# Diagonal blocks of a chunked RWKV-7 scan: one strided transfer instead of sixteen, and the triangular steps on GpSimd instead of VectorE

## The chip, the cores and the metric

The kernel runs on one core of one Trainium2 chip, as a single program. The metric is the device time of one execution in microseconds (us). A core has five engines with queues of their own: TensorE (PE in the profile, its weight loads PEld), VectorE (DVE), ScalarE (ACT), GpSimd (POOL) and SyncE (SP, which here only issues transfers). Each engine takes its instructions strictly in the order in which they stand in its queue; an instruction that has to wait for a semaphore holds everything behind it on that engine. Transfers are issued by SP, ACT or POOL and moved by 16 DMA engines.

## The reference

A decoder trunk of two layers on 512 tokens and 16 learned meta tokens, width 1024. Each layer is: half-step SwiGLU block, a mixer (a 31-tap convolution branch beside an RWKV-7 branch, both gated), a second half-step SwiGLU block, each followed by a LayerNorm. What the change touches is the RWKV-7 scan in the mixer, 16 heads of size 64:

```python
def step(S, inp):
    r_t, w_t, k_t, v_t, kk_t, a_t = inp
    sa = jnp.einsum("bhvk,bhk->bhv", S, -kk_t)
    S = (S * w_t[:, :, None, :]
         + sa[..., None] * (kk_t * a_t)[:, :, None, :]
         + v_t[..., None] * k_t[:, :, None, :])
    y = jnp.einsum("bhvk,bhk->bhv", S, r_t)
    return S, y
...
_, ys = lax.scan(step, S0, xs)
```

The state S of a head is 64x64; every token applies a rank-one correction to it and adds a rank-one term. All numbers are float32.

## The kernel before

The scan is computed in chunks of 64 tokens (`C`, eight of them, `NCH`) and a first chunk of the 16 meta tokens (`NM`). Inside a chunk the corrections of the tokens depend on each other through a 64x64 triangular matrix with ones on its diagonal, one for each head and chunk, and its inverse is needed before the chunk can be scanned.

The 16 heads go in four quarters (`q`) of four heads, and a quarter's 32 matrices in two halves (`g`) of four chunks, 16 matrices each. For a quarter the work is:

- `prep` projects and prepares the operands of two pairs of heads.
- `scores` makes, chunk by chunk on PE (L1345, L1354), the matrices. ACT copies the triangular part to the tile `ut` (L1359), and SP writes it to a scratch tensor `mscr` in DRAM (L1366).
- `substitution(q, g)` inverts the 16x16 diagonal blocks of a half: four per matrix, 64 in all (68 in the first half, with the meta chunk's), one on each partition. SP fetches them from `mscr` to the tile `im` (L1380), DVE does 15 columns with one multiplication (L1389, into `is`) and one addition (L1392, on `ix`) each, 30 dependent instructions. ACT copies the transposed result to `it` (L1396). SP writes both to `xdscr` in DRAM (L1398) and fetches them back into the block diagonals of `dd` (L1403), 16 transfers of 8 KB: two forms, four blocks, two groups of partitions. What lies beside the blocks in `dd` was set to zero once per layer (L1143).
- `inverse(q, g)` puts the 64x64 inverses together on PE from `ut` and `dd` (16 products at L1428, then three rounds of 16 at L1435, with DVE between), and ACT copies them to `G` (L1442).
- `scan(q)` goes through the eight chunks (L1510 to L1545). While it runs, the scores of the next quarter are made, and with them the first half's `substitution` of that quarter. That quarter's first `inverse` comes after the scan, its second one at the start of its own scan.

So each layer has eight substitutions and eight inverses. The four first halves of a layer are called the "first-half places" below, eight in the kernel. They have the short way from scores to inverse; the second halves are needed only when the next scan begins.

PE is kept busy between these steps by other products of the mixer, projections of 264 columns each (`mm` at L250, 48 of them to a projection); the text calls them fill. DVE has the convolution's taps (`cacc`, L1183) and the splitting of weights (`w_lo`, L164) as its own filling work. POOL sets tiles and issues the accumulating transfers of part of the weight splits (L158 in the mixer).

The order of the instructions on each engine is made when the program is built, by a scheduler that takes them by priority and by the times it expects of them. The priorities of taps and scores are shifted by `high_priority`; otherwise nothing in the code fixes where on PE an inverse stands. `nosync` adds an order without a wait; `self.hold` is the instruction that the next tap has to come after in that order.

Of the kernel before, what the change touches and what calls it, by code (L numbers as in the profile page):

```python
# [11 lines left out]
ALU = mybir.AluOpType  # L12
# [4 lines left out]
P = 128  # L17
# [3 lines left out]
NM = 16  # L21
# [8 lines left out]
HS = 64  # L30
C = 64
NCH = SEQ // C
LN_EPS = 1e-5
GN_EPS = 64e-5
ALPHA = (2 * DEPTH) ** 0.25
# [72 lines left out]
class Trunk:  # L108
# [686 lines left out]
    def mixer(self, l, last, pre, more):  # L795
        nc, tc = self.nc, self.tc
        self.l, self.last = l, last
        self.t0, self.n = (NM, SEQ // 2) if last else (0, T // 2)
        dram = lambda name, shape: self.dp.tile(shape, F32, name=f"{name}{l}")
# [3 lines left out]
        self.gs = dram("gscr", [2 * D, T])  # L803
        self.us = dram("uscr", [D, T])
        self.ds, self.as_, self.ggs = dram("dscr", [D, T]), dram("ascr", [D, T]), dram("ggscr", [D, T])
        self.ms = dram("mscr", [4, NCH * 4, C, C])
        self.ms0 = dram("mscr0", [4, 4, NM, NM])
        self.xs0 = dram("xscr0", [4, 4, NM, NM])
        self.xd = dram("xdscr", [4, 2, 2, P // 2, NM, NM])
        ppool, self.pp = self.enter(f"mix_ps{l}", space=PSUM)  # L810
        pms = [self.mm() for _ in range(2)]
        self.glu0 = self.sc()
# [55 lines left out]
        N = prep(1)  # L868
        post = iter(())
        self.cuts = CUTS  # L870
        for q in range(4):
# [42 lines left out]
            Q, N = N, prep(q + 2) if q < 2 else None  # L914
# [147 lines left out]
    def mixer_begin(self, zs, filler):  # L1062

        nc, mp, d = self.nc, self.mp, self.d
        z = self.tmp()
        self.token_mix(zs[0], 24, z)
        nc.scalar.activation(z[0:64, :], z[0:64, :], AF.Tanh)
        x = self.tmp("kp", 1, F32R), self.tmp("k2", 1, F32R)  # L1070
        self.split(z, *x)
        z = self.tmp()
        self.token_mix(zs[1], 25, z)
        nc.scalar.activation(z, z, AF.Tanh, scale=0.5)
        xg = self.tmp("a", 1, F32R), self.tmp("pinv", 1, F32R)
        nc.scalar.activation(xg[0], z, AF.Copy, bias=1.0)
        nc.vector.scalar_tensor_tensor(xg[1], z, 1.0, xg[0].bitcast(F32), op0=ALU.add,
                                       op1=ALU.subtract)
        filler(START[0])
        acts = (lambda o: (AF.Sigmoid, self.v1("w0", o), 1.0),  # L1080
                lambda o: (AF.Tanh, self.half[:, 0, o:o + 1], 0.5))
        up = [(d["w_up"], slice(0, 64)), (d["a_up"], slice(64, P))]

        room = mp.tile([P, 4, KT, P], F32R, name="sb", bufs=1)
        w = self.wunit(*((r, u[self.l].rearrange("r (o c) -> r o c", c=P)) for u, r in up),
                       dst=[room[:, 0], room[:, 1]])

        self.bi = 0
        stage = {}

        def lowrank(w, x, o, r, dst, act=None):
            if act is None:
                t = self.tmp("v", 4) if o % 2 else mp.tile([P, NCH * 4, 32], F32, name="b4",
                                                           bufs=B4)
                t = t if o % 2 else t.rearrange("p a b -> p (a b)")[:, 0:T]
            else:
                if o == 0:
                    stage[r.start] = self.rows().rearrange("p q e f t -> p (q e f) t")
                t = stage[r.start][:, o]
            both = self.sc() if self.bi % 2 == 0 else None  # L1100
            self.bi += 1
            for h in range(2):
                s = slice(h * (T // 2), (h + 1) * (T // 2))
                pm = (self.sm(("tr", "ch")[h]) if both is None else both[:, h])[:, :T // 2]
                for j, (a, b) in enumerate(((0, 0), (0, 1), (1, 0))):
                    nc.tensor.matmul(pm, w[a][r, o, :], x[b][r, s], start=j == 0, stop=j == 2)
                to = t[:, s]
                if both is not None:
                    if h == 0:
                        continue  # L1110
                    pm, to = self.pv(both), self.tv(t)
                if act is None:
                    nc.vector.tensor_scalar_mul(to, pm, 0.5)
                else:
                    f, b, scale = act(o)
                    nc.scalar.activation(to, pm, f, bias=b, scale=scale)
            nc.sync.dma_start(out=dst[o * P:(o + 1) * P, :], in_=t)

        wg = self.wunit(d["g_up"][self.l].rearrange("r (o c) -> r o c", c=P),
                        dst=[room[:, 2], room[:, 3]])  # L1120
        todo = [[lambda o=o, r=r, act=act, dst=dst: lowrank(w, x, o, r, dst, act)
                 for o in range(KT)]
                for (_, r), act, dst in zip(up, acts, (self.ds, self.as_))]
        todo.append([lambda o=o: lowrank(wg, xg, o, slice(0, P), self.ggs) for o in range(KT)])
        for i, (j, o) in enumerate(LOW):
            todo[j][o]()
            if i % LOWSTEP == LOWSTEP - 1:
                filler(1)
            self.taps(TAP0[0])
        filler(START[1])  # L1130
        self.sb = mp.tile([P, NCH, 4, 2 * C], F32, name="sb", bufs=1)

        self.ut = mp.tile([P, NCH * 2, C], F32, name="ut")

        small = mp.tile([P, 2048], F32, name="small")
        nc.gpsimd.memset(small, 0.0)
        self.small, o = {}, 0
        for name, n in (("kb", 512), ("s", 256), ("v", 256), ("u", 256), ("y0", 256), ("y1", 256), ("y2", 256)):
            self.small[name] = small[:, o:o + n]
            o += n  # L1140

        self.dd = mp.tile([P, NCH * 2, 2, C], F32, name="dd")
        nc.gpsimd.memset(self.dd, 0.0)  # L1143


    def glu_b(self, ct):
# [162 lines left out]
    def scores(self, q, Q):  # L1309


        nc, mp = self.nc, self.mp
# [13 lines left out]
        for e in range(2):  # L1326
            p0 = ps[e][0:NM, 0:4 * 2 * NM].rearrange("a (p f x) -> a p f x", p=2, f=2)
            r = slice(HS * e, HS * e + HS)
            for p in range(2):
                for f in range(2):  # L1330
# [7 lines left out]
                              in_=s0[0:NM, e, :, 1, 0, :])  # L1338
        yield
        for c in range(NCH):  # L1340
# [8 lines left out]
            U = self.ut[C * (c % 2):C * (c % 2) + C, 4 * (c // 2):4 * (c // 2) + 4, :]  # L1349
            pairs = []  # L1350
            for p in range(2):
                for e in range(2):
                    r = slice(HS * e, HS * e + HS)
# [9 lines left out]
            nc.vector.tensor_tensor(G[0:C, :, :, 0, cs].rearrange("a p e t -> a e p t"),  # L1363
                                    pv[0:C, :, :, 0, :], mask[0:C, 0], op=ALU.mult)
            to = 4 * (4 * (c // 4) + 2 * (c % 2) + c % 4 // 2)
            nc.sync.dma_start(out=self.ms[q, to:to + 4].rearrange("h j t -> j h t"), in_=U)  # L1366
            yield

    def substitution(self, q, g, Q):


        nc, mp, dd = self.nc, self.mp, self.dd
        N = NCH * 2
        blocks = [slice(NM * b, NM * b + NM) for b in range(4)]
        np_ = 4 * N + (4 if g == 0 else 0)
        M, X, XT = (mp.tile([P, NM, NM], F32, name=x, bufs=2)[0:np_] for x in ("im", "ix", "it"))
        nc.gpsimd.memset(X, 0.0)
        nc.gpsimd.memset(X.rearrange("s t i -> s (t i)")[:, 0::NM + 1], 1.0)
        for b, r in enumerate(blocks):
            nc.sync.dma_start(out=M[b * N:(b + 1) * N], in_=self.ms[q, g * N:(g + 1) * N, r, r])  # L1380
        if g == 0:
            nc.sync.dma_start(out=M[4 * N:], in_=self.ms0[q])
        steps = []
        for j in range(NM - 1):
            w, k = NM - 1 - j, j + 1
            y = mp.tile([P, 64], F32, name="is", bufs=2)[0:np_, 0:w * k]
            y = y.rearrange("s (t i) -> s t i", t=w)
            x = X[:, j + 1:, 0:k]
            steps.append(nc.vector.tensor_tensor(  # L1389
                y, M[:, j, j + 1:, None].to_broadcast([np_, w, k]),  # L1390
                X[:, j, None, 0:k].to_broadcast([np_, w, k]), op=ALU.mult))
            steps.append(nc.vector.tensor_tensor(x, x, y, op=ALU.add))  # L1392
        for later, earlier in zip(steps[1:], steps):
            self.nosync(later, earlier)
        self.hold = steps[-1]
        nc.scalar.copy(XT, X.rearrange("s t i -> s i t"))  # L1396
        for f, x in enumerate((X, XT)):
            nc.sync.dma_start(out=self.xd[q, g, f], in_=x[0:4 * N])  # L1398
            for b, r in enumerate(blocks):
                for e in range(2):  # L1400
                    o = C * e + NM * b
                    k = b * N + e * N // 2
                    nc.sync.dma_start(out=dd[o:o + NM, g * N // 2:(g + 1) * N // 2, f, r],  # L1403
                                      in_=self.xd[q, g, f, k:k + N // 2]
                                      .rearrange("s t i -> t s i"))
        if g == 0:
            nc.sync.dma_start(out=self.xs0[q], in_=XT[4 * N:])
            xt0 = mp.tile([P, 64], F32, name="xt", bufs=1)[0:NM].rearrange("a (s t) -> a s t", s=4)
            nc.sync.dma_start(out=xt0, in_=self.xs0[q].rearrange("s i t -> i s t"))
            Q["xt0"] = xt0  # L1410
# [401 lines left out]
```

## Time and profile before

| | |
|---|---|
| median of 3 runs | 3013.95 us (3011.65 to 3015.38) |
| the profiled execution | 3008.79 us, its span 3007.1 us |
| mean granted PE clock in it | 0.994 |
| PE busy | 2936.7 us, 98% of the span |
| DVE busy | 2272.8 us, 76% |
| ACT busy | 1417.0 us, 47% |
| POOL busy | 181.4 us, 6% |
| the two mixers | about 400 to 960 us and 1910 to 2490 us |

A view of groups gives busy time, mean duration and what ended the idle time ahead of the group. A timeline row has start and duration in us, engine, line, operation, tiles and count, and in brackets the idle time of the engine ahead of it and what ended it. SPq rows are issues: their duration is the time that SP took to issue, not that of the transfer. A row of windows gives for each stretch its length, busy time and count of each engine, the granted PE clock, the share of the DMA engines and GB/s.

### The profile page before, as it was taken

What the parts mean: (1) busy time and instruction counts of PE and PEld (TensorE: products, weight loads), DVE (VectorE), ACT (ScalarE), POOL (GpSimd) and SP (SyncE); (2) the same over time, 40 slices, a digit from 0 to 9 for tenths busy, and PEclk for the clock granted to TensorE, in tenths of its full rate; (3) what the DMA queues carried; (4) which work ended last, traced back from release to release, by engine and by line L of the source; (5) the groups of instructions that cost most, each with busy time, mean ns of one, the idle gap of its engine ahead of it and who ended that gap; (6) DMA issues with size and microseconds to landing.
All of it is one profiled execution on the core that took longest, in us unless ns stands there. A gap on an engine that the chain in (4) does not pass through costs nothing. (4 is left out here: it accounts for less than half of the span.)

```text
span 3007.1 us, 64793 instructions
## 1 busy us (share of the span) xinstructions
PE 2936.7 (98%) x26420; PEld 2809.8 (93%) x26420; DVE 2272.8 (76%) x4657; ACT 1417.0 (47%) x2513; POOL 181.4 (6%) x288
## 2 busy tenths in 40 slices
PE   9999999999999999999999999999999989999998
PEld 8999989888888999999999999898888879999998
DVE  5776778998887768676776767789888777677767
ACT  4444444354555534444444444543444564355543
POOL 1110000000000000100001000000000000001100
PEclk9999999999999999999999999999999999999999
DMA  7565534435455645565555654444354656456651
GB/s 193 139 158 129 130 108 154 109 100 128 107 151 140 186 141 131 136 149 127 130 131 137 148 134 123 132 143 106 90 132 104 169 139 194 125 142 147 149 145 56
DMA packets 556152, 405.33 MB, mean 135 GB/s; under 512 B 89306, under 2 KB 500798, under 8 KB 555854
## 3 DMA queue, kind: packets, MB, share of 16 engines
q1 hardware_dynamic: 520302, 308.49, 36.0%
q0 software_dynamic: 30944, 84.18, 15.2%
q10 hardware_dynamic: 4608, 8.52, 0.8%
q8 instruction: 208, 3.41, 0.5%
q14 instruction: 90, 0.74, 0.1%
HBM read 270.81 MB, written 47.12 MB: 106 GB/s over the span
## 5 line engine op out<-in xcount | busy, mean ns | idle before, releaser
L218 PE MATMUL mm<-xh,w_hi 128*128 128x264 f32 (+1 forms) x1792 | 509.3, 286 | 13.0 <-ACT xh L463 8.7
L218 PE MATMUL mm<-xl,w_hi 128*128 128x264 f32 (+1 forms) x1792 | 509.4, 285 | 0.6 <-DVE xl L464 0.3
L218 PE MATMUL mm<-xh,w_lo 128*128 128x264 f32 (+1 forms) x1792 | 508.3, 284 | 0.0
L218 PE MATMUL mm<-hh,w_hi 128*128 128x264 f32 (+1 forms) x1408 | 399.6, 284 | 2.5 <-ACT hh L121 2.5
L218 PE MATMUL mm<-hh,w_lo 128*128 128x264 f32 (+1 forms) x1408 | 399.7, 284 | 0.0
L218 PE MATMUL mm<-hl,w_hi 128*128 128x264 f32 (+1 forms) x1408 | 399.3, 284 | 0.2
L250 PE MATMUL mm<-xh,w_hi 128*128 128x264 f32 x1760 | 387.2, 295 | 4.8 <-DVE tmp L1056 1.9
L250 PE MATMUL mm<-xl,w_hi 128*128 128x264 f32 x1760 | 379.8, 293 | 0.0
L1183 DVE SCALAR_TENSOR_TENSOR cacc<-cu,cw,cacc 128x528 f32<-128x528 f32 (+1 forms) x480 | 356.7, 753 | 3.6
L218 PEld LDWEIGHTS mm<-xh,w_hi 128*128 128x128 f32 x1792 | 336.6, 189 | 17.9 <-ACT xh L463 11.7
L218 PEld LDWEIGHTS mm<-xl,w_hi 128*128 128x128 f32 x1792 | 339.2, 189 | 2.9 <-DVE xl L464 2.4
L218 PEld LDWEIGHTS mm<-xh,w_lo 128*128 128x128 f32 x1792 | 338.8, 189 | 0.1
L131 ACT CAST w_hi<-sums 128x512 fp32r<-128x512 f32 (+1 forms) x204 | 154.6, 759 | 313.0 <-PE mm L218 201.7
L250 PEld LDWEIGHTS mm<-xh,w_hi 128*128 128x128 f32 x1760 | 279.4, 190 | 14.9 <-DVE tmp L1056 2.3
L250 PEld LDWEIGHTS mm<-xl,w_hi 128*128 128x128 f32 x1760 | 278.1, 190 | 7.2 <-issue 0.2
L218 PEld LDWEIGHTS mm<-hh,w_hi 128*128 128x128 f32 x1408 | 264.7, 188 | 3.1 <-ACT hh L121 2.9
L218 PEld LDWEIGHTS mm<-hl,w_hi 128*128 128x128 f32 x1408 | 264.9, 188 | 0.9 <-DVE hl L122 0.8
L218 PEld LDWEIGHTS mm<-hh,w_lo 128*128 128x128 f32 x1408 | 265.4, 189 | 0.1
L250 PE MATMUL mm<-xh,w_lo 128*128 128x264 f32 x1760 | 262.1, 292 | 0.0
L155 ACT CAST w_hi<-w_raw 128x1024 fp32r<-128x1024 f32 x130 | 136.2, 1050 | 257.3 <-PE mm L218 77.6
L164 DVE TENSOR_TENSOR w_lo<-w_raw,w_hi 128x1024 fp32r<-128x1024 f32 (+1 forms) x194 | 201.5, 1042 | 64.2 <-ACT w_hi L155 60.3
L250 PEld LDWEIGHTS mm<-xh,w_lo 128*128 128x128 f32 x1760 | 229.6, 189 | 6.4
(375 smaller groups left out, 6672.0 us busy)
## 6 DMA issues: line engine op xcount, KB each, us to landing
w_raw<-in_w_in_dram SPq DMA_DIRECT2D x116, 512.0 KB
w_lo<-w_raw POOLq DMA_DIRECT2D x100, 512.0 KB, 5.1
w_raw<-in_ffn_wg_dram SPq DMA_DIRECT2D x88, 512.0 KB
w_raw<-in_ffn_wu_dram SPq DMA_DIRECT2D x88, 512.0 KB
w_raw<-in_ffn_wd_dram SPq DMA_DIRECT2D x80, 512.0 KB
w_lo<-w_raw POOLq DMA_DIRECT2D x68, 256.0 KB, 3.6
w_raw<-in_conv_wo_dram SPq DMA_DIRECT2D x16, 512.0 KB
w_raw<-in_rwkv_wo_dram SPq DMA_DIRECT2D x16, 512.0 KB
```

Of the source, the lines that this page charges most:

```text
L131: self.nc.scalar.copy(hi, x)
L155: copy = self.nc.scalar.copy(hi[:, :kt], raw[:, :kt])
L164: sub = self.nc.vector.tensor_tensor(lo[:, k], raw[:, k], hi[:, k].bitcast(F32), op=ALU.subtract)
L218: self.issued = self.nc.tensor.matmul(pm, a[:, k, :], b[:, xk + k, s], start=first and k == 0 and j == 0, stop=last and k == nk - 1 and j ...
L250: m = self.issued = self.nc.tensor.matmul(pm[:, h, :n], a[:, wk + k, :], b[:, xk + k, s:s + n], start=first and i == 0, stop=last and i == ...
L1183: tap = nc.vector.scalar_tensor_tensor(y, x, w, y, op0=ALU.mult, op1=ALU.add)
```

## The change

The scratch tensors get a padded layout: a 64x64 matrix takes 4160 words instead of 4096 (`DIAG` is 16 x 65 and a matrix has four of them), so that the four diagonal blocks of a matrix lie at one constant stride, 1040 words, and so do those of all 16 matrices of a half. Hence:

- the fetch of the blocks to `im` is one transfer instead of four;
- the two results are written to `xdscr` by one transfer each, as before, now straight onto the diagonals (rows of 64 bytes instead of 1 KB);
- `dd` is fetched whole, zeros included, by two transfers of 128 KB for each form, four instead of sixteen;
- `xdscr` is one tensor for both layers and all quarters, and is set to zero once, in layer 0, by two transfers issued by POOL from the zeroed `dd`; the setting of `dd` to zero in layer 1 goes.

The 30 instructions of each substitution go from DVE to POOL, 480 in all, and `self.hold` is with them an instruction of POOL.

```diff
+DIAG = NM * (C + 1)
...
-        self.ms = dram("mscr", [4, NCH * 4, C, C])
+        self.ms = dram("mscr", [4, NCH * 4, 4 * DIAG])
...
-        self.xd = dram("xdscr", [4, 2, 2, P // 2, NM, NM])
+        if l == 0:
+            self.xd = dram("xdscr", [2, 2, NCH * 2, 4 * DIAG])
...
         self.dd = mp.tile([P, NCH * 2, 2, C], F32, name="dd")
-        nc.gpsimd.memset(self.dd, 0.0)
+        if self.l == 0:
+            nc.gpsimd.memset(self.dd, 0.0)
+            zero = self.dd.rearrange("p s f i -> p (s f i)")
+            xd = self.xd.rearrange("g f r z -> (g f r) z")
+            for a in range(2):
+                nc.gpsimd.dma_start(out=xd[:, a * C * C // 2:(a + 1) * C * C // 2],
+                                    in_=zero[a * C:(a + 1) * C])
...
-            nc.sync.dma_start(out=self.ms[q, to:to + 4].rearrange("h j t -> j h t"), in_=U)
+            nc.sync.dma_start(out=self.ms[q, to:to + 4, 0:C * C]
+                              .rearrange("h (j t) -> j h t", t=C), in_=U)
...
+    @staticmethod
+    def diagonal(x):
+        x = x.rearrange("r (b z) -> (r b) z", b=4)[:, 0:NM * C]
+        return x.rearrange("p (t i) -> p t i", i=C)[:, :, 0:NM]
...
-        for b, r in enumerate(blocks):
-            nc.sync.dma_start(out=M[b * N:(b + 1) * N], in_=self.ms[q, g * N:(g + 1) * N, r, r])
+        nc.sync.dma_start(out=M[0:4 * N], in_=self.diagonal(self.ms[q, g * N:(g + 1) * N]))
...
-            steps.append(nc.vector.tensor_tensor(
+            steps.append(nc.gpsimd.tensor_tensor(
                 y, M[:, j, j + 1:, None].to_broadcast([np_, w, k]),
                 X[:, j, None, 0:k].to_broadcast([np_, w, k]), op=ALU.mult))
-            steps.append(nc.vector.tensor_tensor(x, x, y, op=ALU.add))
+            steps.append(nc.gpsimd.tensor_tensor(x, x, y, op=ALU.add))
...
         for f, x in enumerate((X, XT)):
-            nc.sync.dma_start(out=self.xd[q, g, f], in_=x[0:4 * N])
-            for b, r in enumerate(blocks):
-                for e in range(2):
-                    o = C * e + NM * b
-                    k = b * N + e * N // 2
-                    nc.sync.dma_start(out=dd[o:o + NM, g * N // 2:(g + 1) * N // 2, f, r],
-                                      in_=self.xd[q, g, f, k:k + N // 2]
-                                      .rearrange("s t i -> t s i"))
+            nc.sync.dma_start(out=self.diagonal(self.xd[g, f]), in_=x[0:4 * N])
+        for f in range(2):
+            rows = self.xd[g, f, :, 0:C * C].rearrange("(e s) (t i) -> e t s i", e=2, i=C)
+            for e in range(2):
+                nc.sync.dma_start(out=dd[C * e:C * e + C, g * N // 2:(g + 1) * N // 2, f],
+                                  in_=rows[e])
```

The scheduler puts many instructions in another order. Two places matter below. In the rows of the changed kernel the line numbers are its own; tiles and shapes tell which row is which.

On PE, the last quarter of layer 0, from just ahead of its first inverse (`sc<-dd,ut` is L1428 before; `mm` rows are fill). Before:

```order
L250 MATMUL mm<-xl,w_hi 128x264 x2
L250 MATMUL mm<-xh,w_lo 128x264 x16
L1428 MATMUL sc<-dd,ut 64x64
L250 MATMUL mm<-xh,w_hi 128x264 x2
L250 MATMUL mm<-xl,w_hi 128x264
L1428 MATMUL sc<-dd,ut 64x64 x15
```

The same place after, here from the last scores of the quarter (`sc<-G,FB`) on:

```order
L1362 MATMUL sc<-G,FB 128x128 x4
L251 MATMUL mm<-xl,w_hi 128x264
L251 MATMUL mm<-xh,w_lo 128x264 x16
L251 MATMUL mm<-xh,w_hi 128x264 x2
L251 MATMUL mm<-xl,w_hi 128x264 x2
L251 MATMUL mm<-xh,w_hi 128x264
L1439 MATMUL sc<-dd,ut 64x64
```

The inverse now stands 22 fill products behind the last scores, where 138 stood between them before. Counted from the scores of the fourth chunk, whose matrices are the last that the first half needs, the fill products ahead of the inverse are, at the eight first-half places in turn, 188, 191, 152, 174, 200, 172, 150 and 149 before and 102, 93, 65, 72, 104, 76, 66 and 72 after: 91 fewer on average. The other products between the two (scores, scan) are the same to within a few.

On ACT, the third quarter of layer 0, around the transposing copy `it<-ix`, which waits for the last of the 30 steps. Before:

```order
L1463 COPY small<-ch 16x256
L153 CAST w_hi<-w_raw 128x512 x2
L1347 COPY sb<-sc 128x4x64
L1359 COPY ut<-sc 64x2x2x64
L1195 ACTIVATE glus<-mm 128x528
L1197 DMA gscr_4672<-glus 128x528
L1396 COPY it<-ix 68x256
```

The same place after (`sb`, `ut` are the copies out of the scores' product, `w_hi` a fill weight):

```order
L1540 COPY va<-ch 64x256
L1409 COPY it<-ix 68x256
L1355 COPY sb<-sc 128x4x64
L1467 COPY small<-tr 16x256
L1556 COPY b_8876<-ch 64x256
L1367 COPY ut<-sc 64x2x2x64
L1474 COPY small<-ch 16x256
L154 CAST w_hi<-w_raw 128x512 x2
```

The copy that waits for the steps now stands ahead of the last two chunks' copies and of a fill weight's cast; before, it stood behind them.

More of the change, by code (lines that the diff above doesn't have):

```diff
@@ L1373, in substitution @@
         N = NCH * 2
-        blocks = [slice(NM * b, NM * b + NM) for b in range(4)]
         np_ = 4 * N + (4 if g == 0 else 0)
```

## The prediction

> **What bounds the kernel.** I read the page's first part, then PE's waits, and then the timeline from scores to inverse.
>
> ```profile
> PE 2936.7 (98%) x26420; PEld 2809.8 (93%) x26420; DVE 2272.8 (76%) x4657; ACT 1417.0 (47%) x2513; POOL 181.4 (6%) x288
> ```
>
> PE is the bound: 70 us of its span are idle. So no engine's relief counts by itself; only PE's waits and PE's clock do. Of the waits that this change can touch, the view of waits (us in all, times, longest) has three lines:
>
> ```profile
> PE sc L1428 <- DMA dd<-xdscr: 6.9, 3, 4.7
> PE sc L1435 <- DMA dd<-xdscr: 3.6, 3, 2.8
> PE tr L1510 <- DVE sv L1539: 3.1, 9, 0.8
> ```
>
> Nearly all of the first two is in the last quarters of the layers, and behind each wait PE's clock drops (PE's timeline; then windows, whose third column from the right is the granted clock):
>
> ```profile
> 918.73 0.30 PE L1428 MATMUL sc<-dd,ut 64*64 64x64 f32 x2 [2.01 <-DMA dd<-xdscr]
> 927.74 0.29 PE L1435 MATMUL sc<-dd,b 64*64 64x64 f32 x2 [2.83 <-DMA dd<-xdscr]
> 2411.39 0.45 PE L1428 MATMUL sc<-dd,ut 64*64 64x64 f32 x2 [4.74 <-DMA dd<-xdscr]
> ...
> 919.00:923.00 4.00, 4.00 (x41) 3.74 (x41) 4.00 (x12) 0.74 (x1) 0.84 (x1) 0.57 1.11 231
> 929.00:937.00 8.00, 8.00 (x94) 7.01 (x91) 3.67 (x13) 1.08 (x3) 0.00 (x0) 0.57 0.37 120
> 2411.00:2418.00 7.00, 6.62 (x50) 6.17 (x51) 5.74 (x16) 0.00 (x0) 0.00 (x0) 0.51 0.40 93
> ```
>
> The waits are 2.0 + 2.8 + 4.7 = 9.6 us. The low clock costs 4 x 0.43 = 1.7, 8 x 0.43 = 3.4 and 7 x 0.49 = 3.4, together 8.5, or 2.8 us for one wait of 2 to 5 us. If the way to the inverse got shorter and nothing else changed, 18 us would be to be had, no more.
>
> **The way from scores to inverse.** The third quarter of layer 0 is a first-half place at which PE does not wait today. SP's timeline, DVE's first and last step, and PE:
>
> ```profile
> 770.75 0.72 PE L1354 MATMUL sc<-G,FB 64*128 64x128 f32 x8
> ...
> 774.18 1.79 SPq L1380 DMA_DIRECT2D im<-mscr  x4
> 777.73 0.58 SPq L1366 DMA_DIRECT2D mscr<-ut  x1
> ...
> 779.96 0.40 SPq L147 DMA_DIRECT2D w_raw<-in_w_in_dram  x1
> ...
> 794.97 0.48 SPq L1398 DMA_DIRECT2D xdscr<-ix  x1
> ...
> 797.09 8.55 SPq L1403 DMA_DIRECT2D dd<-xdscr  x16
> ...
> 807.30 1.19 SPq L147 DMA_DIRECT2D w_raw<-in_w_in_dram  x2
> ...
> 779.86 0.15 DVE L1389 TENSOR_TENSOR is<-im,ix 68x15 f32<-68x15 f32 x1
> 794.74 0.17 DVE L1392 TENSOR_TENSOR ix<-ix,is 68x15 f32<-68x15 f32 x1
> ...
> 801.25 0.41 PE L250 MATMUL mm<-xl,w_hi 128*128 128x264 f32 x2
> 801.50 1.87 PE L250 MATMUL mm<-xh,w_lo 128*128 128x264 f32 x14
> 803.30 0.33 PE L1428 MATMUL sc<-dd,ut 64*64 64x64 f32 x2
> ```
>
> The scores of the fourth chunk end at T = 771.5. The steps begin at T + 8.4 and end at T + 23.4: 15.0 us, of which 30 x 0.2 = 6 are the steps themselves and the rest is other DVE work in between. PE is at the inverse at T + 31.8.
>
> **The change, part by part.**
>
> *The inverse stands earlier on PE.* Two fill products take 0.245 us (801.25 to 801.50). Here 72 stand ahead of the inverse instead of 174: 102 x 0.1225 = 12.5 us earlier, so PE arrives at T + 19.3. (The mean over the eight places, 91 products, is 11.1 us.) The fill isn't lost, it comes later; but if the inverse isn't ready at T + 19.3, PE stands still, since its order is fixed.
>
> *Transfers.* One fetch to `im` instead of four: 1.79 becomes about 0.58 (the row of one `mscr` issue of 64 KB), 1.2 us earlier. The first form's eight `dd` issues take half of 8.55 us, 4.3; two issues take 1.2: 3.1 earlier. Against that, 256 KB go where 64 KB went, and `xdscr` is written in 64-byte rows. The page's part 6 prices bytes:
>
> ```profile
> w_lo<-w_raw POOLq DMA_DIRECT2D x100, 512.0 KB, 5.1
> w_lo<-w_raw POOLq DMA_DIRECT2D x68, 256.0 KB, 3.6
> ```
>
> 256 KB more cost 1.5 us there, so 192 KB more cost at most 1.1; I take 0.8, and 0.4 for the small rows (bounds 0 and 2: a fetch to `im` has such rows already and is used 4 us behind its last issue, 775.97 to 779.86). From the last row of `ix` to the landed first form of `dd` it took 2.2 us to the first `dd` issue, 4.3 of issues, and about 0.9 of landing (at the place in layer 1, half of the 16 issues of 7.41 us that follow ends at 2410.5 and PE goes on at 2411.39).
>
> ```profile
> 2406.79 7.41 SPq L1403 DMA_DIRECT2D dd<-xdscr  x16
> ```
>
> After, it is 2.2 + 1.2 + 0.9 + 0.8 + 0.4 = 5.5. With S the duration of the 30 steps, the operand is there at T + (8.4 − 1.2) + S + 5.5 = T + 12.7 + S, and PE waits S − 6.6 us. What decides is S.
>
> *The steps on POOL.* The trace has no POOL operation with two inputs. Groups by form give the price against the size, POOL's timeline the time between two:
>
> ```profile
> L291 POOL TENSOR_SCALAR_AFFINE_SELECT mskb<-mskb 64x16 f32<-64x16 f32 x8 | 1.3, 196 | 0.0
> L280 POOL TENSOR_SCALAR_AFFINE_SELECT msk<-msk 64x64 f32<-64x64 f32 x4 | 0.9, 234 | 0.1
> L1378 POOL MEMSET ix<- 68x16 f32 x8 | 1.0, 122 | 0.3
> L158 POOL DMA_DIRECT2D w_lo<-w_raw x32 | 27.1, 847 | 413.4 <-ACT w_lo L157 200.8 <-ACT b L1545 66.5 <-ACT w L1512 34.5
> ...
> 567.57 0.31 POOL L1377 MEMSET ix<- 68x256 f32 x1 [37.47 <-DMA xdscr<-ix]
> 567.93 0.12 POOL L1378 MEMSET ix<- 68x16 f32 x1
> ```
>
> A step has 15 to 64 elements on a partition, 45.3 on average (680 in 15). By the selects that is 196 + 0.79 x 29.3 = 219 ns; a second input that costs as much as the first adds 45.3 x 0.79 = 36; and 0.05 us lie between two instructions (567.88 to 567.93). So 0.305 us, S = 9.2. The lower bound goes by the 122 ns memset: 30 x 0.172 = 5.2. The upper bound has to allow that POOL and DVE get into each other's way at SBUF, on which the trace says nothing. DVE's two-input work in the eight windows from scores to inverse (the sums of `cacc`, and of `w_lo` beside it):
>
> ```profile
> sum 281.00, DVE 81.94 ACT 0.00; mean DVE 10.24 ACT 0.00
> sum 281.00, DVE 26.01; mean DVE 3.25
> ```
>
> If every such instruction held the steps up for its whole length, a window would add 10.24 + 3.25 = 13.5: S = 22.7. I take 9.2, which goes by the row nearest in kind.
>
> The wait is then 2.6 us at each of eight places, 21 us, each with a low clock behind it at 2.8 us, 22. The three old waits, 18 us, are in this and go. Sum: 21 + 22 − 18 = +25 on the profiled 3008.8: 3034. The median of the runs shown is 5 above the profiled run: 3039, and I say 3040.
>
> **What is queued behind.** Each POOL step waits for the one before. Ahead of and behind them stand the `w_lo` issues of L158, 0.85 us each, which are late by up to S; they wait mostly for ACT today, 200.8 us in all, and feed fill that comes well later: nothing. On ACT the transposing copy waits for the last step, ahead of the last two chunks' copies; the steps end at T + 16.4, within a few us of when those copies are due, and the second half's inverse has some 20 us to spare: nothing at S = 9. On SP the writes to `xdscr` wait for POOL and hold the next `mscr` writes and weight fetches; SP issues no `w_raw` here between 779.96 and 807.30 anyway: nothing. What it costs where these covers are too thin is rival E.
>
> **DVE is rid of** 480 steps of 0.198 us:
>
> ```profile
> L1389 DVE TENSOR_TENSOR is<-im,ix x240: 154/198/223, 554.2 to 2428.3; 68x15 f32<-68x15 f32 x16, 68x39 f32<-68x39 f32 x16, 68x55 f32<-68x55 f32 x16, 68x63 f32<-68x63 f32 x16
> ```
>
> That is 95 us on an engine that is busy for 76%. PE waited 3.1 us for DVE in the scan (L1539 above); at most that comes back, and I count nothing. The two transfers of zeros in layer 0 lie long before the first inverse, and the memset that goes in layer 1 was POOL's: nothing.
>
> **Rivals.**
>
> A, the forecast: waits of about 1 to 4.5 us at most places; 3020 to 3060.
>
> B, the steps collide with DVE at SBUF. For it: in the windows DVE is busy for 244 of 281 us, and two-input taps and splits are 108 us of it, a share of 0.38.
>
> ```profile
> sum 281.00, PE 270.69 PEld 245.28 DVE 244.12 ACT 126.80 POOL 6.82; mean PE 33.84 PEld 30.66 DVE 30.51 ACT 15.85 POOL 0.85
> L1183 DVE SCALAR_TENSOR_TENSOR cacc<-cu,cw,cacc 128x528 f32<-128x528 f32 (+1 forms) x480 | 356.7, 753 | 3.6
> ```
>
> A step that meets a tap with chance 0.38 and waits out half of its 0.753 us loses 0.14: 30 x 0.14 = 4.3, S = 13.5. The wait is 6.9 x 8 = 55, with the clock 22, less 18: +59, 3073 by the median; at the bound S = 22.7 it is 16.1 x 8 = 129, and 3147. Against it: no row shows such a collision. The Trainium skill states it as a rule ("SBUF — State Buffer", section "Who interferes with whom"): a DVE instruction with two inputs in SBUF contends with a GpSimd instruction that reads SBUF, as an exclusive lock under which the later one fully blocks. No run here has shown it yet; by that rule the time is that of this rival.
>
> C, faster: the steps are done before PE comes. S below 6.6 decides, that is 0.22 us a step, and the selects without a second input's cost give 0.219 + 0.05. Then no new wait, and the old ones go: 3013.95 − 18 = 2996; if half of the old waits stay, 3005. For it: the rest of the way is certain to get shorter, and POOL has little else to do meanwhile. Since each place has its own slack, single waits may stay.
>
> D, no change: S near 7.5. Waits of 0.9 us at eight places, too short for the clock to fall everywhere, against the 18: 3008 to 3020.
>
> E, the backlog: the copy on ACT and the writes on SP, held by the steps, make the scores of the last two chunks late, so that PE waits there too, up to 2.5 us at eight places: +20 on A, 3060. It needs S above 10.
>
> **How the numbers follow.** A 0.36, B 0.24, C 0.25, D 0.08, E 0.07. About 0.2%, 6 us, is what a measurement of this kernel can tell from no change. Faster is C, 0.25; the same is D, 0.08; slower A, B and E, 0.67. The range reaches to C's better end, 2996, less 1 us, and into B up to S = 16.5, 9.9 x 8 + 22 − 18 = +83, 3097, rounded to 3100; what is left out is a few hundredths below and one tenth above. A's own range is 3020 to 3060.
>
> **What would show it.** In the profile after: the eight first `sc<-dd,ut` rows with waits of 1 to 5 us for `dd<-xdscr` and a clock near 0.55 behind; POOL's busy time up by 480 x 0.25 = 120 us; the 30 steps lasting 9 us; `im` and each `dd` form with one and two issues. Steps of 0.2 us in median but with a tail as long as a tap, or taps longer than 753 ns, speak for B; rows without a wait at these places for C. The step most likely to be wrong is S, on which one us more or less is 8 us of time; next is the landing of `dd`, where a 64-byte row that costs more than I take moves all eight places too.

## The result, and the profile after

| | before | after |
|---|---|---|
| median | 3014.66 us (3011.65 to 3017.43, 4 runs) | 3089.27 us (3086.42 to 3091.23, 4 runs) |
| ratio to before | | 1.0249 (95% interval 1.0235 to 1.0262) |
| profiled execution, its span | 3008.79, 3007.1 us | 3086.42, 3084.7 us |
| mean granted PE clock | 0.994 | 0.981 |
| PE busy; idle in the span | 2936.7; 70.4 us | 2954.5; 130.2 us |

The change costs 75 us where 26 were forecast. The span is 77.6 us longer: PE is idle for 59.8 us more, and its busy time is 17.8 us more for the same 26420 products, at a lower granted clock. The first part of the page of after:

```profile
PE 2954.5 (96%) x26420; PEld 2827.9 (92%) x26420; DVE 2210.8 (72%) x4177; ACT 1417.9 (46%) x2513; POOL 360.0 (12%) x769
```

PE's waits of after (us in all, times, longest). L1362, L1355, L1409 and L1405 of after are the second scores product, the copy to `sb`, the copy `it<-ix` and the step's addition:

```profile
PE sc L1362 <- ACT sb L1355: 37.3, 5, 9.4
PE sc L1259 <- ACT tmp L1257: 14.4, 6, 5.0
PE ch L1471 <- ACT b L1556: 13.3, 2, 6.7
PE ch L1543 <- ACT va L1540: 9.5, 6, 7.4
...
PE sc L1247 <- ACT tmp L1232: 3.8, 1, 3.8
```

The two lines for `dd` of before are gone; PE doesn't wait for `dd` any more. What PE waits for is ScalarE. At the third quarter of layer 0, the place of the prediction's sum, ACT's timeline, then PE's and SP's:

```profile
798.04 0.37 ACT L1540 COPY va<-ch 64x256 f32<-64x256 f32 x1 [0.94 <-PE ch L1537]
805.02 0.62 ACT L1409 COPY it<-ix 68x256 f32<-68x256 f32 x1 [6.62 <-POOL ix L1405]
805.67 0.37 ACT L1355 COPY sb<-sc 128x256 f32<-128x256 f32 x1
...
806.10 1.23 PE L1362 MATMUL sc<-G,FB 64*128 64x128 f32 x8 [6.59 <-ACT sb L1355]
...
797.00 0.59 SPq L1649 DMA_DIRECT2D bon<-bscr  x1
805.02 0.58 SPq L1411 DMA_DIRECT2D xdscr<-ix  x1
```

The transposing copy stands at the head of ACT's queue and waits 6.62 us for the last step; the copy `sb` of the sixth chunk, long due, is behind it; PE's next scores wait for that copy. SP stands at its write of `ix` for the same reason. The eight first-half places have one such wait each, for a copy that stands behind `it<-ix` on ACT: 8.68, 6.24, 6.59, 7.39, 9.40, 6.39, 6.74 and 6.61 us, 58.0 in all. Behind each the clock falls (a window of PE's clock right behind the first wait; third column from the right):

```profile
566.70:572.80 6.10, 6.10 (x30) 5.88 (x31) 2.96 (x5) 1.42 (x2) 0.43 (x2) 0.50 0.66 120
```

That is 6.1 x 0.5 = 3 us lost, near the 2.8 that the prediction took; in the 6 us behind the eight waits the granted clock is 0.50 to 0.72, together 21.5 us lost. And the steps themselves: POOL's timeline, with DVE's beside it.

```profile
796.12 0.28 POOL L1402 TENSOR_TENSOR is<-im,ix 68x55 f32<-68x55 f32 x1
796.48 1.03 POOL L1405 TENSOR_TENSOR ix<-ix,is 68x55 f32<-68x55 f32 x1
797.59 0.72 POOL L1402 TENSOR_TENSOR is<-im,ix 68x60 f32<-68x60 f32 x1
798.38 0.30 POOL L1405 TENSOR_TENSOR ix<-ix,is 68x60 f32<-68x60 f32 x1
...
795.93 0.43 DVE L1369 TENSOR_TENSOR sb<-sc,msk 128x256 f32<-128x256 f32 x1
796.27 0.41 DVE L1371 TENSOR_TENSOR G<-sc,msk 64x256 f32<-64x256 f32 x1
796.61 1.55 DVE L1191 SCALAR_TENSOR_TENSOR cacc<-cu,cw,cacc 128x528 f32<-128x528 f32 x2
```

While DVE masks the scores out of PSUM (796.27) a step of 55 elements takes 0.28 us. While DVE runs two taps (796.61 to 798.16) the next two take 1.03 and 0.72, and each ends about 0.15 us behind the end of a tap. Then a step of 60 takes 0.30 again. Sorting all 480 steps of after by what DVE ran at the same time:

| DVE meanwhile | steps | mean of a step |
|---|---|---|
| nothing | 257 | 262 ns |
| taps or weight splits (two inputs in SBUF) | 111 | 682 ns |
| other work, most of it with an input in PSUM | 112 | 299 ns |

The first row is the step's own price: 215 ns at 15 elements, 302 at 64. Between two steps lie 78 ns. So 30 steps take 30 x 0.262 + 29 x 0.078 = 10.1 us alone, and in the first halves S, the time from the first step to the end of the last, was 12.6 us (11.6 to 13.5). That is not longer than before: on DVE, with other work between the steps, the same eight chains took 13.5 us on average (10.9 to 15.1). What has changed is how early PE, ACT and SP come to their result. The taps hardly paid for the collisions (the group's mean; before it was 753 ns):

```profile
L1191 DVE SCALAR_TENSOR_TENSOR cacc<-cu,cw,cacc 128x528 f32<-128x528 f32 (+1 forms) x480 | 356.8, 756 | 6.0 <-ACT cacc L1189 2.1
```

### The profile page after: what moved, and what is told of

Same layout as the page of the kernel before. It is cut to its first block, busy times and chain, and to the rows that moved or that the text cites. A ratio compares the mean times of both kernels' runs of the same rounds, so it can differ in the third digit from the quotient of the medians.

```text
span 3084.7 us, 64400 instructions
## 1 busy us (share of the span) xinstructions
PE 2954.5 (96%) x26420; PEld 2827.9 (92%) x26420; DVE 2210.8 (72%) x4177; ACT 1417.9 (46%) x2513; POOL 360.0 (12%) x769
## 4 chain that ended last, share of the span: by engine, by line
PE 55%; DVE 4%; DMA 2%; POOL 2%; ACT 1%; issue 1%; SPq 0%; ACTq 0%; DVEq 0%; POOLq 0%
PE mm L219 42%; PE mm L251 8%; POOL is L1402 1%; POOL ix L1405 1%; PE sc L1446 1%; DVE cacc L1191 1%; DVE y L454 1%; DMA im<-mscr 1%; DVE ln_rstd L448 1%; DVE w_lo L165 0%; PE sc L1362 0%; PE ch L1543 0%; PE tr L1521 0%; DVE xl L465 0%; DMA mscr<-ut 0%
## 5 line engine op out<-in xcount | busy, mean ns | idle before, releaser
L219 PE MATMUL mm<-xh,w_hi 128*128 128x264 f32 (+1 forms) x1792 | 509.4, 286 | 13.1 <-ACT xh L464 9.1
L251 PE MATMUL mm<-xl,w_hi 128*128 128x264 f32 x1760 | 386.6, 296 | 0.0
L219 PEld LDWEIGHTS mm<-xh,w_hi 128*128 128x128 f32 x1792 | 336.6, 189 | 17.8 <-ACT xh L464 12.1
L219 PEld LDWEIGHTS mm<-xl,w_hi 128*128 128x128 f32 x1792 | 339.2, 189 | 3.2 <-DVE xl L465 2.6
L251 PEld LDWEIGHTS mm<-xh,w_hi 128*128 128x128 f32 x1760 | 285.2, 194 | 10.6 <-DVE tmp L1058 2.3
L251 PEld LDWEIGHTS mm<-xl,w_hi 128*128 128x128 f32 x1760 | 284.8, 194 | 6.7 <-issue 0.4
L251 PE MATMUL mm<-xh,w_lo 128*128 128x264 f32 x1760 | 270.1, 296 | 2.5 <-DMA w_lo<-w_raw 2.5
L165 DVE TENSOR_TENSOR w_lo<-w_raw,w_hi 128x1024 fp32r<-128x1024 f32 (+1 forms) x194 | 201.9, 1049 | 89.5 <-ACT w_hi L156 59.8
```

What stands on the lines that cost most here:

```text
L165: sub = self.nc.vector.tensor_tensor(lo[:, k], raw[:, k], hi[:, k].bitcast(F32), op=ALU.subtract)
L219: self.issued = self.nc.tensor.matmul(pm, a[:, k, :], b[:, xk + k, s], start=first and k == 0 and j == 0, stop=last and k == nk - 1 and j ...
L251: m = self.issued = self.nc.tensor.matmul(pm[:, h, :n], a[:, wk + k, :], b[:, xk + k, s:s + n], start=first and i == 0, stop=last and i == ...
```

## The experiments

All ratios are to the kernel before, run beside, with 95% intervals.

**The two parts apart.** e1_dma_only has the new transfers and the steps on DVE; e2_pool_only the old transfers and the steps on POOL.

```diff
-            steps.append(nc.gpsimd.tensor_tensor(
+            steps.append(nc.vector.tensor_tensor(
```

> The steps go back to VectorE, the new transfers stay. The inverse stands 139 fill products behind the fourth chunk's scores on average (172 before, 79 with both changes): 4 us earlier than before, while the way to it is 3 us shorter. Theory (the long steps on GpSimd make the loss): 3000 to 3020, with no wait of 6 us at any first-half place. Rival (the rows of 64 bytes, or 256 KB for the block diagonals, make it): 3025 to 3090, with waits for dd.

> The steps go to GpSimd, the transfers stay as before. The inverse stands 104 fill products behind the fourth chunk's scores. Theory: steps of 13 us again, waits of 5 to 8 us for ScalarE's copies or for dd at the eight places, 3060 to 3095. Rival (the transfers): 3010 to 3030.

e1: 3005.86, ratio 0.9963 (0.995 to 0.9975), faster by 0.37%. e2: 3079.85, ratio 1.0209 (1.0195 to 1.0223). The transfers alone gain 11 us, and the steps on POOL alone lose 62. The two don't add up: both together lose 75, more than e2, so that with the steps on POOL the new transfers gain nothing. The inverse stands 104 fill products behind the scores in e2 and 79 after, where it stood at 172 before and stands at 139 in e1. Moving the steps thus moved PE's order as well, in e2 too, and no run has the steps on POOL with the whole order of before. In e1 the last quarters kept waits for `dd` of 6.3 and 6.1 us, which I had not expected: PE comes there earlier too.

**Where the wait is seen.** e3 takes the copy off ACT, e4 leaves it there but, in the first halves, puts it and what follows behind the last chunk's copies.

```diff
-        nc.scalar.copy(XT, X.rearrange("s t i -> s i t"))
+        nc.gpsimd.tensor_copy(XT, X.rearrange("s t i -> s i t"))
```

For e4, the code from that copy on is called behind the last scores, with

```diff
+        it = nc.scalar.copy(XT, X.rearrange("s t i -> s i t"))
+        if g == 0:
+            self.nosync(it, self.utcopy)
```

> Both changes, but the transposing copy `it<-ix` is GpSimd's, so nothing on ScalarE waits for the steps; PE's order is as after (inverse at 82 products on average). Theory (PE's place for the inverse is too early for steps of 13 us; ScalarE only decides where the wait is seen): the waits at the scores go, and PE waits about 6 us for dd at each inverse instead: 3060 to 3095. Rival (ScalarE held up by the copy is the loss itself): 3010 to 3035.

> Both changes, but for the first halves the copy `it<-ix` and the writes and fetches behind it are put behind the last chunk's `ut` copy on ScalarE; the inverse stays at 83 products. Theory: no wait at the scores in the first halves, 4 to 6 us for dd at the inverse instead: 3050 to 3090. Rival (ScalarE held up is the loss itself): 3010 to 3035.

e3: 3106.58, ratio 1.0295 (1.0278 to 1.0311); e4: 3128.85, ratio 1.0364 (1.0338 to 1.0389). In e3 the waits at the scores are gone and PE waits at the inverse, 11.4 us on average at the eight places (PE's waits of e3):

```profile
PE sc L1439 <- DMA dd<-xdscr: 92.3, 12, 17.4
```

The wait only moves, as the theory said; but both end above the range it gave, e4 far above: it has 82.5 us of waits for `dd`, and 32.9 more for copies `small` that ScalarE makes late. S is 17.5 us in e3 (first halves) and 16.3 in e4: when PE isn't stopped at the scores, DVE goes on with taps beside the steps (168 steps meet a tap or split in e3, 111 after). After, ACT's queue starves DVE of work and so shortens the steps: at each of the eight places DVE is idle for 6.5 to 9.3 us, until a copy comes that stood behind `it<-ix`. At the third quarter (DVE's timeline of after):

```profile
806.72 1.22 DVE L1581 TENSOR_REDUCE gn_st<-b 128x16 f32<-128x1024 f32 x1 [8.56 <-ACT b L1556]
```

In e3, while the steps run, DVE has no wait of more than 3.4 us at these places.

**Is it the taps?** Both on e3. e5 turns the order between the last step and the next tap into a wait, e6 leaves 29 of 30 taps out, so that its result isn't the convolution.

```diff
-                self.nosync(tap, self.hold)
+                self.sync(tap, self.hold)
```

```diff
+            if j < TAPS - 1:
+                yield True
+                continue
             tap = nc.vector.scalar_tensor_tensor(y, x, w, y, op0=ALU.mult, op1=ALU.add)
```

> The kernel with the copy on GpSimd (3107), but the next convolution tap on VectorE really waits for the last of the 30 steps (so far it is only ordered behind it, which means nothing across two engines). Theory (taps hold up the steps at SBUF: steps of first halves last 17.5 us, 9 without a tap beside them): steps of 9 to 12 us, waits at the inverse of 4 to 7 us instead of 11.4, 3050 to 3080. Rival (steps slow for another reason): steps of 16 us or more and 3095 to 3115.

> The same kernel, with 29 of the 30 taps of VectorE left out of each convolution block, so that its result isn't the convolution. Its inverses stand 11 fill products earlier still, 1.3 us. Theory: steps of 9 to 10.5 us in the first halves, waits of 4 to 6 us, 3040 to 3070. Rival (the steps' length is GpSimd's own): 17 us, 3100 or more.

e5: 3081.5, ratio 1.0221 (1.0206 to 1.0236), S 10.9 us. e6: 3071.39, ratio 1.0181 (1.0162 to 1.02), S 13.0 us. In e5 the steps are as short as expected and the kernel gains 25 us on e3, a little less than expected: taps that wait hold DVE's other work up, and PE now waits 34 us in six waits for a mask at the scores. e6 ends a little above its range too, and its steps stayed longer than the 9 to 10.5 I expected. Freed of taps, DVE brings its weight splits and other two-input work into the same stretch: the 20 splits that meet a step last 872 ns on average and the 22 steps that meet a split 827, and PE's waits for `dd` are still 82.1 us in all. The length follows what DVE has in SBUF at the time, not the tap as such; GpSimd's own part is the 264 ns of the 266 steps that met nothing.

**A later inverse.** e7 (on e3) and e8 (on e1) give the first halves' inverses a priority 300 lower; e9 is e7 with the meta chunk's products lowered as well (at the first quarters both by 240).

```diff
-                self.inverse(q + 1, 0, N)
+                with self.tc.high_priority(offset=-300):
+                    self.inverse(q + 1, 0, N)
```

> The kernel with the copy on GpSimd, but the first halves' inverses have a priority 300 lower, and stand 174 fill products behind the fourth chunk's scores on average instead of 82: 11 us later, as in the kernel before. The steps stay on GpSimd. Theory (the loss is PE's early arrival against steps of 13 to 17 us): the waits for dd go but for 1 to 4 us in the last quarters, 3005 to 3030. Rival (GpSimd's steps cost elsewhere, by slowing VectorE or holding GpSimd's transfers): 3060 or more.

> The new transfers with the steps on VectorE (3006), and the same lower priority for the first halves' inverses: 170 fill products instead of 139. The waits of 6.3 and 6.1 us in the last quarters get 2 to 3 us shorter and the small ones go: 2992 to 3004. Rival (a later inverse delays the scan and makes waits there): 3006 to 3020.

> As the kernel with the later inverse (3162), but the meta chunk's products, which read `xt` out of the same steps' result and at which PE then stood for 81 us in all, get the lower priority too (240 at the first quarters, 300 at the others); the inverse stands 170 fill products behind the fourth chunk's scores on average. Theory (PE only stands where its order comes to a consumer of the steps too early): those 81 us go to under 15, and what stays is the price of a later scan, as in the kernel with the transfers alone and a later inverse (48 us above its own base): 3040 to 3075. Rival (with steps on GpSimd the way itself is longer, wherever the consumers stand): 3100 or more, with waits for xt or dd of 8 us.

e7: 3161.95, ratio 1.0489 (1.0473 to 1.0506). e8: 3054.38, ratio 1.0129 (1.0108 to 1.015). e9: 3122.77, ratio 1.0359 (1.0338 to 1.038). All three missed. In e7 PE waits 81.3 us for `xt`, another result of the same steps that the meta chunk reads: I had moved one of two consumers. In e9 that wait is gone and those for `dd` are 15.0 us, as expected, but there are others (PE's waits of e9):

```profile
PE sc L1448 <- DVE b L1442: 20.4, 5, 5.7
PE sc L1441 <- DMA dd<-xdscr: 15.0, 11, 3.3
PE mm L251 <- DMA w_lo<-w_raw: 15.0, 3, 8.7
```

The inverse's rounds wait for DVE, and fill waits for weights; the `w_lo` transfers are POOL's, behind the steps. e8 shows the price of a late inverse without POOL. Its idle time is that of e1 to within 4 us, but PE's busy time is 35 us more for the same products. The reading that fits is that fill which is spent ahead of the inverse is missing in the scan behind it. Windows of e8 and of e1 over the scan of the first quarter (length, PE busy and products, ..., granted clock):

```profile
589.00:634.00 45.00, 38.34 (x291) 32.66 (x290) 32.03 (x67) 11.35 (x23) 0.16 (x2) 0.73 0.23 64
```

```profile
589.00:634.00 45.00, 42.43 (x483) 38.39 (x482) 41.85 (x85) 19.55 (x42) 0.73 (x6) 1.00 0.44 121
```

PE looks busy, but with 291 products recorded instead of 483, at a clock of 0.73. So PE's order can't simply be put back by these priorities, and whether some order would suit steps on POOL stays open.

**SyncE's order.** e10 is e1 with the second half's fetch to `im` ordered behind the first half's fetches to `dd`.

```diff
+        if g == 1:
+            self.nosync(fetch, self.placed)
```

> The new transfers with the steps on VectorE (3006), and the fetch of the second half's blocks ordered behind the first half's fetches to `dd` on SyncE. In the last quarters SyncE stood 5.1 us at that fetch while the first half's result was ready. Theory: the waits of 6.3 and 6.1 us there fall to 2 to 4 us, 2996 to 3004. Rival (a transfer of weights ahead in the queue makes them): 3004 to 3010.

e10: 3001.27, ratio 0.9954 (0.9939 to 0.997). The two waits are 4.6 and 4.2 us instead of 6.3 and 6.1, a little above the 2 to 4 expected. The interval overlaps that of e1, so that the gain of this edit alone is not shown.

**First halves or second halves.** e11 has the steps on POOL in the second halves alone, e12 in the first alone.

```diff
+        eng = nc.gpsimd if g == 1 else nc.vector
...
-            steps.append(nc.gpsimd.tensor_tensor(
+            steps.append(eng.tensor_tensor(
```

> The new transfers, with the steps on VectorE in the first halves and on GpSimd in the second halves, whose inverses come 57 us and more behind their scores in most quarters. The first halves' inverses stand at 145 fill products, about as with the transfers alone (139). Theory (steps of 13 us cost only where PE's order has no room for them): no more than 6 us from the kernel with the transfers alone (3006), 2998 to 3012. Rival (GpSimd's steps cost wherever they stand, by the copy that holds up ScalarE and by collisions): half of the loss or near it, 3025 to 3045.

> The other way round: GpSimd in the first halves, VectorE in the second. The inverses stand at 82 fill products, as with both changes. Theory: the eight waits of 6 to 9 us are all there, and the waits of the second halves' stretch (18 us in all, for ScalarE's copies of operands of the next quarter) go: 3060 to 3085. Rival: 3035 to 3055.

e11: 3053.67, ratio 1.0133 (1.0117 to 1.015). e12: 3064.26, ratio 1.0172 (1.0156 to 1.0189). e12 is within its range. e11 contradicts the theory: 48 us more than the transfers alone, with results that are not needed for 20 us and more. PE's largest wait in e11, and ACT at its first place:

```profile
PE ch L1567 <- ACT small L1480: 25.9, 7, 5.9
...
582.13 0.62 ACT L1410 COPY it<-ix 64x256 f32<-64x256 f32 x1 [14.21 <-POOL ix L1406]
582.65 1.04 ACT L156 CAST w_hi<-w_raw 128x1024 fp32r<-128x1024 f32 x1
583.60 0.36 ACT L1480 COPY small<-ch 16x256 f32<-16x256 f32 x1
```

ACT stood 14.2 us at a copy that nobody needed yet, and PE waited for another one behind it.

**The queues that stand at a result.** e13 takes the second halves' copy in e11 to POOL; e14 does so with both changes; e15 is e13 with the second halves' writes and fetches issued by POOL instead of SP; e16 has steps, copy, writes and fetches of both halves on POOL.

```diff
+        if g == 1:
+            nc.gpsimd.tensor_copy(XT, x)
+        else:
+            nc.scalar.copy(XT, x)
```

```diff
+        queue = nc.gpsimd if g == 1 else nc.sync
...
-            nc.sync.dma_start(out=self.diagonal(self.xd[g, f]), in_=x[0:4 * N])
+            queue.dma_start(out=self.diagonal(self.xd[g, f]), in_=x[0:4 * N])
```

> GpSimd's steps in the second halves only, and their transposing copy `it<-ix` on GpSimd too. In the kernel with that copy on ScalarE (3054), ScalarE stood 99 us at it, and PE waited 26 us for a copy `small` behind it. The operand itself has 20 us to spare. Theory (there the copy at the head of ScalarE's queue is the loss): that wait goes, and the time falls to the kernel with the transfers alone, 3000 to 3015. Rival (collisions, or GpSimd's late weight transfers): 3030 or more.

> Both changes, with the second halves' copy `it<-ix` on GpSimd and the first halves' on ScalarE as after. Theory: the first halves' eight waits for ScalarE stay at 6 to 9 us, the second halves' part goes: 3055 to 3070, as with GpSimd in the first halves only (3064). Rival (the second halves' share is not that copy): 3080 to 3095.

> As the kernel with steps and copy of the second halves on GpSimd (3034), and the two writes to `xdscr` and the four fetches to `dd` of the second halves are issued by GpSimd too. In that kernel SyncE stood 97.5 us at the first of these writes, and ScalarE then waited 40.8 us (12.0 with the transfers alone) for weights that SyncE fetched behind it. Theory (what is left of the loss is SyncE's queue): ScalarE's waits for these weights go back to about 12 us and the time to that of the transfers alone, 3000 to 3015. Rival (collisions with VectorE alone, or GpSimd's weight transfers held up): 3028 to 3045.

> Both changes in both halves, with the copy, the writes and all fetches behind the steps on GpSimd's queue, so that neither ScalarE nor SyncE waits for a step. The first halves' inverses stand at 77 fill products, 9.4 us of fill less than with the transfers alone on average (139) and less still than before. Theory: the second halves cost nothing, as just shown; in the first halves PE waits for dd itself at the eight inverses, 9 to 13 us each with steps of 16 to 18 us: 3085 to 3110. Rival (the two queues were all of the loss): 3000 to 3020.

| | median | ratio to before |
|---|---|---|
| e13 | 3033.94 | 1.0069 (1.0053 to 1.0084) |
| e14 | 3084.93 | 1.0235 (1.0218 to 1.0252) |
| e15 | 3002.67 | 0.9959 (0.9944 to 0.9974) |
| e16 | 3102.95 | 1.0295 (1.0271 to 1.0319) |

e13 wins back 20 of e11's 48 us, and e14's interval overlaps that of after: both ended where the rival was expected, and the theory of one queue fell. But collisions alone weren't it either. The first inverses of e11 and e13 stand at the same place on PE. SP's and ACT's waits in e13 show the second one, and the timelines of SP, ACT and PE how it works:

```profile
SPq L1416 <- POOL ix L1406: 97.5, 8, 13.8
...
ACT w_hi L154 <- DMA w_raw<-in_w_in_dram: 40.8, 9, 11.0
...
801.41 0.57 SPq L1425 DMA_DIRECT2D xt<-xscr  x1
815.43 0.59 SPq L1416 DMA_DIRECT2D xdscr<-ix  x1
...
817.85 0.39 SPq L148 DMA_DIRECT2D w_raw<-in_w_in_dram  x1
...
822.75 1.14 ACT L154 CAST w_hi<-w_raw 128x512 fp32r<-128x512 f32 x2 [4.96 <-DMA w_raw<-in_w_in_dram]
823.80 0.61 ACT L1257 COPY tmp<-rs 128x512 f32<-128x512 f32 x1
...
824.46 1.11 PE L1259 MATMUL sc<-ident,tmp 128*128 128x128 f32 x4 [3.60 <-ACT tmp L1257]
```

SP stands from 801.98 to 815.43 at the write of `ix`. The fetch of a weight behind it goes out at 817.85, ACT waits 4.96 us for that weight, and a copy that PE needs (`tmp`) is behind ACT's cast. e15 takes this wait off SP: ACT's waits for these weights fall from 40.8 to 10.6 us (12.0 in e1), and the loss is gone, to within the spread of e1. Its steps in the second halves last 16.6 us on average, longer than after, and still cost nothing measurable: where the result has time, neither the length nor the collisions matter, only which queues stand waiting for it.

This was shown with the first halves on DVE; no run takes SP's wait out of the second halves alone while the first halves are as after.

In the first halves that isn't enough. In e16, which ended within its range, neither ACT nor SP waits for a step, and PE waits at the eight first inverses for 12.3, 12.4, 11.0, 13.6, 13.1, 9.4, 10.7 and 12.7 us (PE's waits of e16):

```profile
PE sc L1439 <- DMA dd<-xdscr: 103.7, 15, 13.6
```

There the steps, 17.3 us long, are on PE's own way. (77 fill products instead of 139 are 7.6 us at 0.1225 each, not the 9.4 that I expected.)

## Why the prediction was wrong

*The direction was right and the time lies within the range, but the size was not right: +26 forecast, +75 measured.* Its steps in turn:

*PE's earlier place, and the formula S − 6.6: right.* With S = 17.3 and 17.5 in e16 and e3 it gives waits of 10.7 and 10.9 us; measured were 11.9 and 11.4 on average. With the S of after, 12.6, it gives 6.0; measured were 7.25, though in front of another product.

*S, the term that failed first: 9.2 forecast, 12.6 measured.* The price of a step alone was nearly right, 0.305 us forecast against 0.262 + 0.078 = 0.340; a second input does cost about as much as the first (1.78 ns for an element more, where the selects had 0.79). POOL's busy time rose by 179 us, not by 120. What I put aside as rival B is real: steps that met a two-input DVE instruction took 682 ns instead of 262. The excess of all steps is 51 us in 16 halves, 3.2 each, where B had 4.3; in the first halves 12.6 − 10.1 = 2.5. Rival C, which went by a cheaper step, was further off: 0.219 + 0.05 is 0.269 us a step, and that was already more than the 0.22 that it needed. The Trainium skill has this rule ("SBUF — State Buffer", section "Who interferes with whom"): a DVE instruction with two SBUF inputs contends with a GpSimd instruction that reads SBUF. The trace agrees on which instructions collide: the 34 steps that met taps alone took 667 ns, those that met masks or additions with an input in PSUM 257 to 268. The same section of the Trainium skill says that the order of issue, and not the kind of instruction, decides who blocks. The trace agrees for most: of 64 steps that began while a tap ran, 61 ended behind that tap, by 150 ns in the median. It doesn't for all: when a tap began, 16 steps were running that nothing had held up until then; 10 of them took 211 to 313 ns, but 6 were held to the tap's end or beyond.

*What is queued behind, costed at nothing: the second failure.* I had ACT's copy, SP's writes and POOL's issues in the list and called each covered, since the result and the late copies had time. It was the other things in those queues that had none. In the first halves this only decided where the same wait is seen. In the second halves, which the sum leaves out altogether, it made a loss of its own: after against e12 25 us (3089 to 3064). With both corrected the sum comes close: 6.0 x 8 = 48, the clock 22, less 18, is +52, and 25 more is +77. Part of that is luck: with the waits as measured, 58 instead of 48, the same terms give +87, and the credit of 18 was too large. The profile's own account is 58.0 us for the eight waits, less the 9.6 of before, 11.4 for all other idle time and 17.8 for busy time, together 77.6.

*Rival E* named the backlog at the right place, but as an addition to A above S = 10 and for the first halves only. *The credit of 18 us:* the transfers alone gave 11 us (e1), where PE comes to the inverse earlier too and the last quarters kept waits of 6 us; with the steps on POOL they gave nothing (e2 against after).

*DVE's relief, the zeros, the memset:* nothing seen of any of them; DVE is busy 62 us less where 95 were forecast, and PE's waits for DVE in the scan are 2.5 us instead of 3.1.

## What to carry to other kernels

Work that is moved to another engine is to be priced by every in-order queue that stands at its result, and by where the new program puts them, not only by its own length and by when the result is needed. Here the steps of the first halves took no longer than before, and PE still came too early for them. In the second halves a copy on ScalarE and a write on SyncE turned steps with 20 us to spare into 48 us, and moving those two, with the fetches behind, to GpSimd's own queue took it back. Before small steps go to GpSimd beside a busy VectorE, count VectorE's instructions with two inputs in SBUF in that stretch; if the steps are on the bound engine's way, keep them on VectorE. The transfers alone, or with the second halves on GpSimd's own queue, are about 0.4% faster than before (e1, e10, e15).

## What the runs showed of the hardware

A GpSimd step of 15 to 64 elements on 68 partitions with two inputs took 215 to 302 ns and 78 ns to the next one that depends on it. A step that began beside a convolution tap, which has two inputs in SBUF, was in nearly all cases (61 of 64) held to just behind that tap's end. A step that was running freely when the tap began went through in 10 cases and was held in 6. The taps beside a step lasted 771 ns on average, the others 754. In the 6 us behind PE's waits of 6.2 to 9.4 us the granted clock was 0.50 to 0.72. The stall depends on the rest of the kernel: what holds ScalarE holds VectorE's supply, and the steps get shorter (12.6 us after, 17.5 when ScalarE didn't stand at the copy).
